# One core: experts' weights split in an order of their own, differential attention's step b moved, modulation moved behind the merge

## The chip, the cores and the metric

The kernel runs on one core of a Trainium2 chip. The metric is the device time of one execution in microseconds (us); lower is better. The engines have these names in the profile: PE is TensorE (matmuls), PEld its weight loads, DVE is VectorE, ACT is ScalarE, POOL is GpSimd, SP is SyncE, which here only starts transfers. Each engine has its own queue of instructions and works through it in order; semaphores make one wait for another.

## What is computed

A transformer in two parts, all in float32. The first part (`first_block`) has two layers over 1024 tokens and, in the first layer, 256 tokens of context, with a model width of 1024. Reduced to what matters here:

```python
for l in range(2):
    mod = s_c @ ada_w[l] + ada_b[l]                 # six vectors of 1024 for the tokens
    mod_c = s_cc @ ada_w[l] + ada_b[l]              # and six for the context
    hx = rms_norm(x, norm1_g[l]) * (1.0 + sc1) + sh1
    hc = rms_norm(xc, norm1_g[l]) * (1.0 + csc1) + csh1
    y_lat, y_ctx = token_mixers(hx, hc, w_in[l], w_out[l], ...)
    x = x + g1 * y_lat
    x = x + g2 * expert_choice_ffn(rms_norm(x, norm2_g[l]) * (1.0 + sc2) + sh2, ...)
    # layer 0 does the same to the context, with cg1 and cg2

def diff_attn_core(q, k, v, lam):                   # one of the token mixers
    s = einsum('bqhmd,bkhmd->bhmqk', q, k) * (DIFF_D ** -0.5)
    a = softmax(s)
    w = a[:, :, 0] - lam * a[:, :, 1]
    return einsum('bhqk,bkhd->bqhd', w, v)

def expert_choice_ffn(x, router_w, wg, wu, wd):     # 16 experts
    aff = softmax(einsum('bnd,de->bne', x, router_w))
    gate, idx = top_k(aff.transpose(0, 2, 1), cap)  # each expert takes 128 tokens, 32 of the context
    xg = x[bidx, idx]
    hid = silu(einsum('becd,edf->becf', xg, wg)) * einsum('becd,edf->becf', xg, wu)
    o = einsum('becf,efd->becd', hid, wd) * gate[..., None]
    return zeros_like(x).at[bidx, idx].add(o)
```

The second part (a gated delta layer and an attention layer with shared latent keys) is not touched.

## The kernel before, in words

The parts of a layer follow one another: norm_in (modulation, norm and the input products), the mixers (diff attention among them), merge (output products, residual, second norm, router), the ranking of the tokens, and the experts. Inside a part the program is written as small steps, and steps of different work are interleaved by hand: a function is cut into a list of steps or into a generator, and the loop that drives the products pops a step between two groups of matmuls. Each engine runs its instructions in the order in which they were written, apart from what a scheduler with priorities moves; a tile's pool has a number of buffers, and a new tile waits until the oldest buffer is free.

**Modulation.** `ada` makes a stretch of `mod` in blocks of 512 columns. A block has three steps: two `part`s with 16 rows of matmul records between them on TensorE (L166) against a 2 MB piece of `ada_w`, and a `total`, in which ScalarE has copied the four partial sums to `adat` (L169), TensorE adds them up with the matrix `sel4` (L177), VectorE adds the bias tile `adab` (L179), and GpSimd starts the transfer to `modd` in memory (L180). GpSimd also starts the load of the bias (L162). Layer 0's first part is made before and inside norm_in, with one step popped per group of products (columns 2048 to 6144). Layer 1's 12 blocks, 36 steps, are made in layer 0's merge: from tile 3 on a step is popped at four places of each tile, and what remains is popped two at a time between the rounds of the ranking.

**Merge.** A tile is 128 tokens; there are ten in layer 0 (eight and two of context) and eight in layer 1. A tile's products are two times 24 matmuls (L917), and its norm writes h (L938 to L940, the half of it on GpSimd) to memory. The ranking (`best`, `choose`) finds each expert's tokens by rounds on VectorE, and `choose` makes the lists of indices by which GpSimd gathers.

**Diff attention.** A unit is 128 queries of one head; it has two score maps. Step a(m) makes the scores of one map on TensorE (S), their extreme on VectorE (L592, a reduce of 128x1280) and the exponential on ScalarE, which also sums up. Step b makes the factor of the second map on VectorE (L598, L599, both tiny), scales the second map by it (L600), and GpSimd adds the first map to it (L601). Steps c and d transpose and multiply by V. `units` runs them as a pipeline: in each turn a(0) of one unit, b of the unit before, a(1), then c and d of older ones.

**Experts.** For each of 16 experts there are three products (gate, up, down) of 1024x1024 weights. float32 is worked in three passes with a high and a low part: ScalarE copies a weight to `wh` (L1165), and `wl` is the difference (L1166), of which VectorE makes three quarters and GpSimd one, by 128x1024 pieces. `weight` loads half a weight (2 MB, SyncE) and splits it, just ahead of the product that uses it; wh and wl have two buffers of half a weight. `product` runs 48 matmuls of 512 columns (L1187), and in layer 0 also the context's matmuls (L1181, in float32, 32 columns of the array), 16 per half. `fetch` gathers the tokens of the expert after next with GpSimd (L1143), and `scatter` adds the result to memory.

## Time and profile before

| | before |
|---|---|
| median of 3 runs | 4869.98 us (4869.22 to 4873.66) |
| the profiled execution: its own time | 4872.44 us |
| its span, first to last instruction | 4870.5 us |
| mean granted TensorE clock | 0.952 |
| norm_in, layer 0 | 0 to 392 us |
| diff attention, layer 0 | 393 to 604 us |
| merge, layer 0: first to last product | 716 to 902 us |
| ranking and rest of the modulation, layer 0 | 902 to 956 us |
| experts, layer 0 | 956 to 1731 us |
| diff attention, layer 1 | 2049 to 2228 us |
| merge, layer 1: products | 2329 to 2453 us |
| experts, layer 1 | 2513 to 3192 us |

The times of the stages are read from the trace of the profiled execution, in microseconds from the start of its span, and so all of them belong to 4872.44 us and not to the median. Busy time of an engine is the time in which one of its instructions ran; a busy share says nothing by itself, since an engine that is not the last to be waited for may stand idle at no cost. The granted clock is a share of TensorE's full clock of 2.4 GHz.

### The profile page before, as it was taken

Reading aid. Unit: us, or ns where it says so; the run is one execution under the profiler, and the core shown is the slowest. Engines: PE = TensorE matmul, PEld = TensorE weight load, DVE = VectorE, ACT = ScalarE, POOL = GpSimd, SP = SyncE. Lnnn points to the kernel's source line nnn. Section 1 sums busy time; section 2 is a strip of 40 time slices with the busy share of each in tenths; the row PEclk is TensorE's granted clock in tenths of the full one; section 3 lists DMA queues with packets and bytes.
Section 4 is the critical chain, followed back from the end, with each engine's and each line's share of the span. In section 5 each row is a group of like instructions: output and inputs, shape, how many; then the busy total and the mean of one; then the engine's idle time right before and its main releaser. Section 6 shows DMA issues by size and latency. Waiting matters only on the chain.

```text
span 4870.5 us, 77258 instructions
## 1 busy us (share of the span) xinstructions
PE 4427.4 (91%) x30151; PEld 3480.5 (71%) x30151; DVE 3183.5 (65%) x6512; ACT 2225.7 (46%) x4037; POOL 1358.2 (28%) x1033
## 2 busy tenths in 40 slices
PE   8998889799999979989959888879999998898899
PEld 4686676476777757867747666658888876787787
DVE  6536877755555566397778998856666663676551
ACT  3326653255555543376336656643333331454330
POOL 2214502244454422162124444412111100022111
PEclk9999899899999989999979999989999999999999
DMA  6422246687878722313548988821111123146757
GB/s 209 159 89 63 60 140 252 217 295 285 291 285 293 279 87 84 103 48 92 202 160 327 329 320 316 309 95 45 36 36 45 41 61 119 56 169 224 191 151 150
DMA packets 333997, 817.14 MB, mean 168 GB/s; under 512 B 32524, under 2 KB 125380, under 8 KB 333632
## 3 DMA queue, kind: packets, MB, share of 16 engines
q1 hardware_dynamic: 228368, 602.22, 34.2%
q0 software_dynamic: 51520, 125.07, 10.9%
q10 hardware_dynamic: 53744, 84.92, 5.0%
q8 instruction: 237, 3.88, 0.3%
q14 instruction: 128, 1.05, 0.1%
HBM read 690.47 MB, written 121.66 MB: 167 GB/s over the span
## 4 chain that ended last, share of the span: by engine, by line
PE 30%; DVE 8%; issue 5%; ACT 4%; DMA 3%; POOL 1%; SPq 0%; ACTq 0%; POOLq 0%; DVEq 0%
PE ps_z L1358 8%; PE ps_m L1187 5%; DVE wl L1166 4%; ACT wh L1165 2%; PE ps_mm L2211 2%; PE ps_S L2119 2%; PE ps_t L2147 1%; PE ps_m L917 1%; PE ps_i L1680 1%; PE ps_i L1694 1%; PE ps_m L1854 1%; PE ps_i L1687 1%; POOL wl L1166 1%; PE ps_t L1482 1%; PE ps_o L1599 1%
## 5 line engine op out<-in xcount | busy, mean ns | idle before, releaser
L1166 DVE TENSOR_TENSOR wl<-w,wh 128x1024 fp32r<-128x1024 f32 x576 | 843.5, 1508 | 179.7 <-ACT wh L1165 179.7
L1165 ACT ACTIVATE wh<-w 128x1024 fp32r<-128x1024 f32 x768 | 754.6, 1050 | 264.0 <-PE ps_m L1187 151.5
L1166 POOL TENSOR_TENSOR wl<-w,wh 128x1024 fp32r<-128x1024 f32 x192 | 535.7, 2825 | 634.9 <-ACT wh L1165 571.1
L1187 PE MATMUL ps_m<-wl,xTh 128*128 128x512 f32 x1024 | 344.6, 411 | 49.0 <-DVE wl L1166 33.6
L1187 PE MATMUL ps_m<-wh,xTh 128*128 128x512 f32 x1024 | 336.2, 410 | 1.4 <-ACT xTh L1133 1.4
L376 PE MATMUL ps_mm<-wh,hh 128*128 128x256 f32 (+1 forms) x928 | 322.5, 350 | 9.3 <-ACT wh L313 6.1
L1187 PE MATMUL ps_m<-wh,xTl 128*128 128x512 f32 x1024 | 325.1, 399 | 0.0
L376 PE MATMUL ps_mm<-wl,hh 128*128 128x256 f32 (+1 forms) x928 | 317.9, 344 | 2.7 <-DVE wl L314 2.6
L376 PE MATMUL ps_mm<-wh,hl 128*128 128x256 f32 (+1 forms) x928 | 316.1, 342 | 0.0
L1358 PE MATMUL ps_z<-hh,wh 128*128 128x350 f32 (+2 forms) x792 | 277.5, 351 | 2.0 <-ACT hh L1291 1.2
L1187 PEld LDWEIGHTS ps_m<-wl,xTh 128*128 128x128 f32 x1024 | 190.0, 192 | 114.4 <-DVE wl L1166 51.9
L1358 PE MATMUL ps_z<-hl,wh 128*128 128x350 f32 (+3 forms) x792 | 268.1, 339 | 0.0
L1358 PE MATMUL ps_z<-hh,wl 128*128 128x350 f32 (+2 forms) x792 | 264.5, 334 | 0.0
L601 POOL TENSOR_TENSOR e<-e,e 128x1280 f32<-128x1280 f32 (+1 forms) x72 | 191.6, 2661 | 188.2 <-DVE e L600 154.8
L1187 PEld LDWEIGHTS ps_m<-wh,xTh 128*128 128x128 f32 x1024 | 188.0, 192 | 64.2 <-issue 14.4
L1187 PEld LDWEIGHTS ps_m<-wh,xTl 128*128 128x128 f32 x1024 | 195.1, 192 | 41.3
L592 DVE TENSOR_REDUCE mx<-ps_S 128x1 f32<-128x1280 f32 (+1 forms) x144 | 196.1, 1366 | 37.0 <-PE ps_S L591 36.3
L376 PEld LDWEIGHTS ps_mm<-wh,hh 128*128 128x128 f32 x928 | 177.3, 192 | 48.0 <-issue 11.0
L376 PEld LDWEIGHTS ps_mm<-wl,hh 128*128 128x128 f32 x928 | 178.5, 192 | 22.4 <-DVE wl L314 4.4
L594 ACT ACTIVATE e<-ps_S,mx 128x1280 f32<-128x1280 f32 (+1 forms) x144 | 177.4, 1233 | 33.2 <-DVE mx L592 22.0
L376 PEld LDWEIGHTS ps_mm<-wh,hl 128*128 128x128 f32 x928 | 177.5, 192 | 18.8 <-issue 0.8
L1187 PE MATMUL ps_m<-wl,hTh 128*128 128x512 f32 x512 | 165.0, 403 | 20.5 <-DVE wl L1166 12.7
(661 smaller groups left out, 10754.0 us busy)
## 6 DMA issues: line engine op xcount, KB each, us to landing
w<-in_exp_w_gate SPq DMA_DIRECT2D x64, 2048.0 KB
w<-in_exp_w_up SPq DMA_DIRECT2D x64, 2048.0 KB
w<-in_exp_w_down SPq DMA_DIRECT2D x64, 2048.0 KB
w<-in_ada_w SPq DMA_DIRECT2D x12, 2048.0 KB
z<-zd POOLq DMA_DIRECT2D x76, 320.0 KB, 4.6
wraw<-in_ada_w SPq DMA_DIRECT2D x38, 512.0 KB
zd<-hi ACTq DMA_DIRECT2D x76, 256.0 KB
zw<-in_t_win SPq DMA_DIRECT2D x64, 256.0 KB
```

What stands on the lines that cost most here:

```text
L376: nc.tensor.matmul(pm[:, o:], hs[i][x][:, k, a * 128:(a + 1) * 128], w[:, k % 2, o:], start=q == 0, stop=q == 23)
L592: nc.vector.tensor_reduce(U["mx"][:, m:m + 1], S[:, :nk], AX.X, OP.min)
L594: nc.scalar.activation(e[:, :nk], S[:, :nk], AF.Exp, scale=-1.0, bias=U["mx"][:, m:m + 1], accum_out=U["sm"][:, m:m + 1])
L601: nc.gpsimd.tensor_add(w[:, :nk], w[:, :nk], U[0][:, :nk])
L917: nc.tensor.matmul(pm, a[:, k], b[:, k], start=k + x == 0, stop=k == 7 and x == 2)
L1165: nc.scalar.activation(wh[:, k], w[:, k], AF.Copy)
L1166: (nc.gpsimd if k == 3 else nc.vector).tensor_sub(wl[:, k], w[:, k], wh[:, k].bitcast(F32))
L1187: nc.tensor.matmul(pm[:, c], X[i][:, half * 4 + k], W[j][:, k, c * 512:(c + 1) * 512], start=half + k + q == 0, stop=half == 1 and k == 3 ...
L1358: nc.tensor.matmul(q[:M, :n], a[:, k % 4], b[:, k, z0:z0 + n], start=k == 0 and x == 0, stop=k == 7 and x == 2)
L1482: nc.tensor.transpose(pt[:r, i * 128:(i + 1) * 128], src[:, tok(t0 + i)[1]], self.ident)
L2119: nc.tensor.matmul(S[:, ks], q[:, i * 128:(i + 1) * 128], k[:, ks], start=x == 0, stop=x == 4)
L2211: nc.tensor.matmul(pm[:, c], a[:, k], b[:, k, c * 512:(c + 1) * 512], start=k + z == 0, stop=k == 7 and z == 2)
```

## The change

There are three edits, in three parts of the first block.

**Modulation.** The block of columns 5120 to 6144 of layer 0 (two blocks of 512) leaves norm_in and is made in the merge, ahead of layer 1's twelve; so 14 blocks, 42 steps, are there instead of 36. Steps are popped between products only from tile 8 on, eight of them; 34 run in the loop behind the last tile. With `late`, the bias is added by a second small matmul with the identity (L180 after), ScalarE copies the sum out (L181), the first `part` of a block is put ahead of the `total` of the block before, the partial sums alternate between the PSUM banks "a" and "m", and the bias tile has two buffers.

**Diff attention.** a(1) moves ahead of b in a turn, and in b the scalar_tensor_tensor and the scaling are issued behind the reduce of a(1) of the next unit (`issue_after`).

**Experts.** A queue `todo` of weight pieces in the order of the products takes the place of `weight`. `split` loads and splits one piece: in layer 0 half a weight, one piece ahead, with two buffers; in layer 1 a quarter (256 rows), three pieces ahead, with five buffers. wl is made on VectorE alone, in 128x2048 pieces, and ScalarE's copy has that shape too. In layer 0 the context's matmuls of both halves run together when a product begins. In layer 1 the bank of the context's sums goes to the transposes, which then have two.

Lines of the kernel after are 4 to 10 larger up to the merge and the gather, and some 25 to 31 larger in the experts: L592 becomes L598, L599 L607, L600 L608, L629 L637, L632 L640, L180 (the store) L184, L940 L948, L1134 L1144, L1143 L1153, L1166 L1191, L1181 L1212, L1197 L1228, L1204 L1235, L1219 L1250.

```diff
-    def ada(self, l, c0, c1, W, load, p, ps, tag, cols=None):
+    def ada(self, l, c0, c1, W, load, p, ps, tag, cols=None, late=False):
...
-                cur["pa"] = ps(tag)
+                cur["pa"] = ps((tag, "m")[late and j // W % 2])
                 if cols is None:
-                    b = cur["b"] = p.tile([2, W], F32, name="adab", bufs=2 if l else 1)
+                    b = cur["b"] = p.tile([2, W], F32, name="adab", bufs=2 if l or late else 1)
...
-            nc.tensor.matmul(pb[:2, :n], self.sel4, cur["t"][:, :n], start=True, stop=True)
+            pb = ps("m" if late else tag)
             b = cur["b"]
-            nc.vector.tensor_add(b[:, :n], pb[:2, :n], b[:, :n])
+            nc.tensor.matmul(pb[:2, :n], self.sel4, cur["t"][:, :n], start=True, stop=not late)
+            if late:
+                nc.tensor.matmul(pb[:2, :n], self.ident[:2, :2], b[:, :n], start=False, stop=True)
+                nc.scalar.activation(b[:, :n], pb[:2, :n], AF.Copy)
+            else:
+                nc.vector.tensor_add(b[:, :n], pb[:2, :n], b[:, :n])
             nc.gpsimd.dma_start(self.modd[l][:, j:j + n], b[:, :n])
...
+            at = len(steps) - 1 if late and steps else len(steps)
+            steps[at:at] = g[:1]
+            steps += g[1:]
...
-        steps = self.ada(0, 2048, 6144, CW, ada_load, p, ps, "mm") if l == 0 else []
+        steps = self.ada(0, 2048, 5120, CW, ada_load, p, ps, "mm") if l == 0 else []
...
                 old[0]["a"](0)
+                old[0]["a"](1)
             if old[1]:
-                old[1]["b"]()
-            if old[0]:
-                old[0]["a"](1)
+                old[1]["b"](old[0] and old[0].get("max"))
...
-            nc.vector.scalar_tensor_tensor(sm[:, 3:4], sm[:, 3:4], self.nlam, sm[:, 0:1], op0=OP.mult, op1=OP.mult)
-            nc.vector.tensor_scalar(w[:, :nk], w[:, :nk], sm[:, 3:4], None, op0=OP.mult)
+            with self.tc.issue_after(behind) if behind else nullcontext():
+                nc.vector.scalar_tensor_tensor(sm[:, 3:4], sm[:, 3:4], self.nlam, sm[:, 0:1], op0=OP.mult, op1=OP.mult)
+                nc.vector.tensor_scalar(w[:, :nk], w[:, :nk], sm[:, 3:4], None, op0=OP.mult)
...
-                ada = self.ada(1, 0, 6144, 512, ada_load, p, ps, "a")
+                for x, c0 in ((0, 5120), (1, 0)):
+                    ada += self.ada(x, c0, 6144, 512, lambda j, n, i, x=x: ada_load(j, n, i, x), p, ps, "a", late=True)
...
-                            if ada and t >= 3 and n in (0, 3, 4, 7):
+                            if ada and t >= 8 and n in (0, 3, 4, 7):
...
-        with self.pool("ex") as p, self.banks("exps", m=3, c=1, t=1) as ps:
+        with self.pool("ex") as p, self.banks("exps", m=3, **(dict(c=1, t=1) if ctx else dict(t=2))) as ps:
...
-                wh, wl = [p.tile([128, 4, 1024], F32R, name=f"w{b}", bufs=2) for b in "hl"]
-                for k in range(4):
-                    nc.scalar.activation(wh[:, k], w[:, k], AF.Copy)
-                    (nc.gpsimd if k == 3 else nc.vector).tensor_sub(wl[:, k], w[:, k], wh[:, k].bitcast(F32))
...
+            G, ahead = (4, 1) if ctx else (2, 3)
...
+            todo = [(name, e, k) for name, e in order for k in range(0, 8, G)]
+            ready = []
+            def split():
...
+                name, e, k = todo.pop(0)
+                if k % 4 == 0:
+                    self.wraw = self.wr.tile([128, 4, 1024], F32, name="w", tag="w")
+                    nc.sync.dma_start(self.wraw, A[name][l, e, k * 128:(k + 4) * 128].rearrange("(k p) f -> p k f", p=128))
+                w = self.wraw[:, k % 4:k % 4 + G]
+                wh, wl = [p.tile([128, G, 1024], F32R, name=f"w{b}", bufs=ahead + (1 if ctx else 2)) for b in "hl"]
+                for i in range(0, G, 2):
+                    nc.scalar.activation(wh[:, i:i + 2], w[:, i:i + 2], AF.Copy)
+                    nc.vector.tensor_sub(wl[:, i:i + 2], w[:, i:i + 2], wh[:, i:i + 2].bitcast(F32))
+                ready.append((w, wh, wl))
...
+                for s in range(0, 8, G):
+                    w, *W = weight()
+                    if ctx and s == 0:
                         pc = U[key + "c"] = ps("c")
-                    for k in range(4 if ctx else 0):
-                        b = half * 4 + k
-                        for g in range(4):
...
+                        for b in range(8):
+                            v = (w, ready[0][0])[b // 4]
+                            for g in range(4):
...
```

**VectorE in layer 1's diff attention.** The rows are in VectorE's order; mx and sm hold a unit's extremes and sums, e a score map. Before, at a place in the middle:

```order
L600 TENSOR_SCALAR e_18593<-e_18593,sm 128x1280
L592 TENSOR_REDUCE mx<-ps_S 128x1
L598 RECIPROCAL sm<-sm 128x2
L599 SCALAR_TENSOR_TENSOR sm<-sm,nlam 128x1
L592 TENSOR_REDUCE mx<-ps_S 128x1
L600 TENSOR_SCALAR e_18645<-e_18645,sm 128x1280
L629 COPY oT<-ps_t 128x128
L592 TENSOR_REDUCE mx<-ps_S 128x1
L632 TENSOR_SCALAR Y<-ps_t,sm 128x64 x2
L598 RECIPROCAL sm<-sm 128x2
L592 TENSOR_REDUCE mx<-ps_S 128x1
```

After, at the same place:

```order
L608 TENSOR_SCALAR e_18207<-e_18207,sm 128x1280
L598 TENSOR_REDUCE mx<-ps_S 128x1
L604 RECIPROCAL sm<-sm 128x2
L598 TENSOR_REDUCE mx<-ps_S 128x1
L607 SCALAR_TENSOR_TENSOR sm<-sm,nlam 128x1
L637 COPY oT<-ps_t 128x128
L608 TENSOR_SCALAR e_18259<-e_18259,sm 128x1280
L640 TENSOR_SCALAR Y<-ps_t,sm 128x64 x2
L598 TENSOR_REDUCE mx<-ps_S 128x1 x2
L604 RECIPROCAL sm<-sm 128x2
L607 SCALAR_TENSOR_TENSOR sm<-sm,nlam 128x1
```

Before, one reduce stands between a scaling and the next scalar_tensor_tensor in one turn and two in the next; after, two stand there in every turn.

**VectorE in layer 1's experts.** rd is an expert's result on its way to memory, ag the hidden values, xTl and hTl low parts of the transposed tokens and hidden values. From one result before:

```order
L1219 SCALAR_TENSOR_TENSOR rd<-ps_m,gate_22018,g_22030 128x1024
L1166 TENSOR_TENSOR wl<-w,wh 128x1024 x2
L1134 TENSOR_TENSOR xTl<-ps_t,xTh 128x512
L1166 TENSOR_TENSOR wl<-w,wh 128x1024 x6
L1204 TENSOR_TENSOR ag<-ag,ps_m 128x512 x2
L1134 TENSOR_TENSOR hTl<-ps_t,hTh 128x512
L1166 TENSOR_TENSOR wl<-w,wh 128x1024 x3
L1134 TENSOR_TENSOR hTl<-ps_t,hTh 128x512
L1166 TENSOR_TENSOR wl<-w,wh 128x1024 x2
L1197 SCALAR_TENSOR_TENSOR ag<-ag,ps_m 128x1024
L1166 TENSOR_TENSOR wl<-w,wh 128x1024
```

And after:

```order
L1250 SCALAR_TENSOR_TENSOR rd<-ps_m,gate_21636,g_21648 128x1024
L1191 TENSOR_TENSOR wl<-w,wh 128x2048 x4
L1235 TENSOR_TENSOR ag<-ag,ps_m 128x512 x2
L1191 TENSOR_TENSOR wl<-w,wh 128x2048 x2
L1144 TENSOR_TENSOR hTl<-ps_t,hTh 128x512 x2
L1191 TENSOR_TENSOR wl<-w,wh 128x2048 x2
L1228 SCALAR_TENSOR_TENSOR ag<-ag,ps_m 128x1024
L1144 TENSOR_TENSOR xTl<-ps_t,xTh 128x512 x2
L1191 TENSOR_TENSOR wl<-w,wh 128x2048 x4
```

An expert has 18 subtracts of 128x1024 on VectorE before (and six on GpSimd, not shown), and 12 of 128x2048 after.

**GpSimd between layer 0's merge and the first gather.** modd is the modulation in memory, adab the bias tile, h and x belong to the merge's tiles. Before, from the last tiles on:

```order
L925 TENSOR_TENSOR x<-x,o 128x512
L180 DMA modd_78<-adab 2x512
L162 DMA adab<-in_ada_b 2x512
L180 DMA modd_78<-adab 2x512
L162 DMA adab<-in_ada_b 2x512
L180 DMA modd_78<-adab 2x512
L940 TENSOR_TENSOR h<-h,B_8227 128x512
L180 DMA modd_78<-adab 2x512
L1143 DMA x<-hd,idx_8681 128x1024
```

After, the rows ahead of the gather; seven more such pairs of store and load stand above them, and the last h above those:

```order
L184 DMA modd_78<-adab 2x512
L162 DMA adab<-in_ada_b 2x512
L184 DMA modd_78<-adab 2x512 x2
L1153 DMA x<-hd,idx_8683 128x1024
L1153 DMA xc<-hc,idx_8687 128x256
```

Before, one store stands between the last h and the gather; after, ten stores and eight loads of bias stand there.

## Rows read from the trace of the kernel before

**Rows 1.** The page's first part: busy time, share of the span, instructions.

```profile
PE 4427.4 (91%) x30151; PEld 3480.5 (71%) x30151; DVE 3183.5 (65%) x6512; ACT 2225.7 (46%) x4037; POOL 1358.2 (28%) x1033
```

**Rows 2.** Busy times by stage: window, length, engines, clock, DMA share, GB/s.

```profile
716.00:902.00 186.00, 179.72 (x928) 123.79 (x927) 129.61 (x353) 56.02 (x115) 38.60 (x39) 0.98 0.72 262
902.00:956.00 54.00, 22.23 (x110) 8.71 (x109) 42.55 (x128) 7.75 (x16) 8.41 (x10) 0.61 0.57 199
956.00:1731.00 775.00, 772.60 (x5694) 543.19 (x5694) 448.59 (x461) 438.11 (x510) 373.77 (x155) 1.00 0.78 278
2513.00:3192.00 679.00, 600.46 (x2557) 458.54 (x2557) 593.37 (x413) 414.63 (x462) 289.46 (x124) 0.97 0.85 311
```

**Rows 3.** Waits, 2520 to 3185: waiter, releaser, us, times, longest.

```profile
PE ps_m L1187 <- DVE wl L1166: 46.3, 41, 4.2
...
PE ps_m L1187 <- POOL wl L1166: 23.2, 39, 2.0
```

**Rows 4.** Groups by line and form, same stretch: busy us, mean ns.

```profile
L1166 DVE TENSOR_TENSOR wl<-w,wh 128x1024 fp32r<-128x1024 f32 x281 | 493.5, 1806 | 19.5 <-ACT wh L1165 19.5
```

**Rows 5.** One line's instructions, same stretch: ns minimum, median, maximum.

```profile
L1166 DVE TENSOR_TENSOR wl<-w,wh x281: 1207/1218/6758, 2522.8 to 3184.5; 128x1024 fp32r<-128x1024 f32 x141
```

**Rows 6.** Timeline, GpSimd and VectorE, 2732 to 2752: start, length in us, instruction.

```profile
2734.96 5.29 POOL L1166 TENSOR_TENSOR wl<-w,wh 128x1024 fp32r<-128x1024 f32 x2
2743.27 2.57 POOL L1166 TENSOR_TENSOR wl<-w,wh 128x1024 fp32r<-128x1024 f32 x1 [3.02 <-ACT wh L1165]
...
2735.68 13.52 DVE L1166 TENSOR_TENSOR wl<-w,wh 128x1024 fp32r<-128x1024 f32 x6
```

**Rows 7.** Timeline of TensorE in layer 0's experts, behind a context batch.

```profile
1201.83 0.73 PE L1187 MATMUL ps_m<-wh,hTh 128*128 128x512 f32 x2
1202.40 0.62 PE L1187 MATMUL ps_m<-wl,hTh 128*128 128x512 f32 x2
```

**Rows 8.** Groups by line: diff attention of layer 0, layer 1, and GpSimd's add.

```profile
L599 DVE SCALAR_TENSOR_TENSOR sm<-sm,nlam 128x1 f32<-128x1 f32 x40 | 24.8, 621 | 0.5
...
L599 DVE SCALAR_TENSOR_TENSOR sm<-sm,nlam 128x1 f32<-128x1 f32 x32 | 25.6, 801 | 0.6
...
L601 POOL TENSOR_TENSOR e<-e,e 128x1280 f32<-128x1280 f32 x29 | 84.1, 2902 | 63.9 <-DVE e L600 48.3 <-PE ps_t L625 6.1 <-PE ps_t L615 5.7
```

**Rows 9.** Timelines of VectorE in the diff attention of layer 1 and layer 0.

```profile
2106.93 1.48 DVE L592 TENSOR_REDUCE mx<-ps_S 128x1 f32<-128x1280 f32 x1
...
2108.53 1.60 DVE L599 SCALAR_TENSOR_TENSOR sm<-sm,nlam 128x1 f32<-128x1 f32 x1
...
2116.79 1.48 DVE L592 TENSOR_REDUCE mx<-ps_S 128x1 f32<-128x1280 f32 x1
...
491.40 1.48 DVE L592 TENSOR_REDUCE mx<-ps_S 128x1 f32<-128x1280 f32 x1
...
500.28 1.48 DVE L592 TENSOR_REDUCE mx<-ps_S 128x1 f32<-128x1280 f32 x1
```

**Rows 10.** Windows of the merge's products alone (L917): five tiles, four tiles.

```profile
766.50:866.30 99.80, 66.19 (x241) 42.05 (x241) 1.00 0.62 224
2379.80:2440.40 60.60, 50.24 (x193) 34.30 (x193) 1.00 0.30 105
```

**Rows 11.** Timeline of GpSimd from the merge's end to the first gather.

```profile
898.88 0.53 POOL L180 DMA_DIRECT2D modd<-adab  x1 [1.52 <-DVE adab L179]
903.91 0.53 POOL L162 DMA_DIRECT2D adab<-in_ada_b  x1 [4.50 <-DMA modd<-adab]
...
920.23 1.66 POOL L940 TENSOR_TENSOR h<-h,B 128x512 f32<-128x512 f32 x1 [1.44 <-issue]
...
949.37 1.04 POOL L1143 DMA_INDIRECT x<-hd,idx  x1 [23.54 <-DVE gate L1106]
```

**Rows 12.** Timeline of TensorE behind the merge: one block of modulation.

```profile
910.97 3.64 PE L166 MATMUL ps_a<-w,csT 128*32 128x512 f32 x16 [2.89 <-DVE adab L179]
915.39 1.86 PE L177 MATMUL ps_a<-adat,sel 128*2 128x512 f32 x2 [0.78 <-ACT adat L169]
```

More of the change, by code (lines that the diff above doesn't have):

```diff
@@ L1 @@
 import math
-from contextlib import ExitStack, contextmanager
+from contextlib import ExitStack, contextmanager, nullcontext
 from itertools import chain
@@ L169, in part, with total @@
                 nc.scalar.activation(t[:, :n], pa[:, :n], AF.Copy)
-        def total(j, n):
+        def total(cur, j, n):
             if cols is not None:
@@ L183, in ada @@
             n = min(W, c1 - j)
-            steps += [lambda j=j, n=n: part(j, n, 0), lambda j=j, n=n: part(j, n, 1), lambda j=j, n=n: total(j, n)]
+            g = [lambda f=f, cur=cur, j=j, n=n, h=h: f(cur, j, n, *h) for cur in [{}] for f, h in ((part, (0,)), (part, (1,)), (total, ()))]
+            at = len(steps) - 1 if late and steps else len(steps)
+            steps[at:at] = g[:1]
+            steps += g[1:]
         return steps
@@ L673, in a, with b @@
             nc.scalar.activation(e[:, n:n + 256], S[:, 768:], AF.Exp, bias=m, accum_out=sm[:, 2:3])
-        def b():
+        def b(behind):
             sm = U["sm"]
@@ L1169, in product @@
-            def product(U, key, x, name, e):
+            G, ahead = (4, 1) if ctx else (2, 3)
+            order = [("exp_w_gate", 0), ("exp_w_up", 0)]
+            for e in range(NE):
+                order += [("exp_w_gate", e + 1)] * (e + 1 < NE) + [("exp_w_down", e)] + [("exp_w_up", e + 1)] * (e + 1 < NE)
+            todo = [(name, e, k) for name, e in order for k in range(0, 8, G)]
+            ready = []
+            def split():
+                if not todo:
+                    return
+                name, e, k = todo.pop(0)
[8 more added lines that the diff above has]
+                ready.append((w, wh, wl))
@@ L1171, in product, with weight @@
+            def weight():
+                split()
+                return ready.pop(0)
+            for _ in range(ahead):
+                split()
+            def product(U, key, x):
                 pm = U[key] = ps("m", 2)
-                pc = None
                 X = U[x]
-                for half in range(2):
-                    w, *W = weight(name, e, half)
-                    if ctx and half == 0:
+                for s in range(0, 8, G):
+                    w, *W = weight()
+                    if ctx and s == 0:
@@ L1185, in product @@
+                    for k in range(G):
+                        b = s + k
                         for q, (i, j) in enumerate(((0, 0), (0, 1), (1, 0))):
                             for c in range(2):
-                                nc.tensor.matmul(pm[:, c], X[i][:, half * 4 + k], W[j][:, k, c * 512:(c + 1) * 512],
-                                                 start=half + k + q == 0, stop=half == 1 and k == 3 and q == 2)
+                                nc.tensor.matmul(pm[:, c], X[i][:, b], W[j][:, k, c * 512:(c + 1) * 512],
+                                                 start=b + q == 0, stop=b == 7 and q == 2)
@@ L1232, in experts @@
                 f()
-            run(product(E[0], "g", "xT", "exp_w_gate", 0), [], 0)
+            run(product(E[0], "g", "xT"), [], 0)
             silu(E[0])
-            run(product(E[0], "u", "xT", "exp_w_up", 0), fetch(1), 0)
+            run(product(E[0], "u", "xT"), fetch(1), 0)
             for e in range(NE):
@@ L1239, in experts @@
                 if e + 1 < NE:
-                    run(product(E[e + 1], "g", "xT", "exp_w_gate", e + 1), steps, 1)
+                    run(product(E[e + 1], "g", "xT"), steps, 1)
                     silu(E[e + 1])
@@ L1244, in experts @@
                         f()
-                run(product(U, "d", "hT", "exp_w_down", e), [], 0)
+                run(product(U, "d", "hT"), [], 0)
                 scatter(U, e)
                 if e + 1 < NE:
-                    run(product(E[e + 1], "u", "xT", "exp_w_up", e + 1), fetch(e + 2) if e + 2 < NE else [], 0)
+                    run(product(E[e + 1], "u", "xT"), fetch(e + 2) if e + 2 < NE else [], 0)
     def h_src(self, t):
```

26 lines of the change are left out of this document (9 added, 17 removed).

## The prediction, made before the changed kernel ran

> **What bounds the kernel now.** I read the page first, then a table of busy times by stage, then, in each stage that the change touches, the waits and the timeline. TensorE is busy for 91% of the span [rows 1], but that is a mean over stages with different limits, and each has to be looked at by itself [rows 2]. In layer 0's experts (775 us) TensorE works for 772.6 us at full clock, so nothing but less TensorE work can shorten them. In layer 1's experts (679 us) it works for only 600.46 us, while VectorE is busy for 593.37 and DMA has a share of 0.85: three engines are near full, and the waits tell which one ends last. They name the low parts of the weights: TensorE waited 46.3 us for wl from VectorE and 23.2 us for wl from GpSimd [rows 3], together 69.5 of its 78.5 us without work. The merge of layer 0 (186 us) is bound by TensorE too (179.72 busy), and the 54 us behind it, in which the tokens are ranked, are a chain of small steps at a granted clock of 0.61. In the diff attention the limit is a loop between TensorE, VectorE, ScalarE and GpSimd, and I read it from VectorE's rows below.
>
> **Layer 1's experts: -66 us.** Every weight is split into wh and wl. 384 subtracts of 128x1024 make wl; GpSimd has every fourth. VectorE's took 1806 ns in the mean [rows 4], but their minimum is 1207 and their median 1218 [rows 5]. So a minority is very long, and the timeline shows where: beside two subtracts of GpSimd (5.29 us) and a third (2.57) VectorE's run of six took 13.52 us instead of 6 x 1.218 = 7.3, and the excess of 6.2 is most of GpSimd's time in that stretch [rows 6]. The two engines subtract one after the other, and handing a quarter to GpSimd buys little: 281 x (1.806 - 1.218) = 165 us of VectorE's time went into waiting. After the change VectorE does all, in 192 pieces of 128x2048, for which I take twice the median, 2.44 us: 468 us. What else it did here is at most 593.37 - 493.5 = 100 us, so VectorE's floor is 568. TensorE's is its 600.46 us at a clock of 0.97, 582 at full clock. DMA's is 0.85 x 679 = 577. All three now lie below the present 679, and the deeper ring (five pieces of 256 rows instead of two of 512, made three ahead) is what lets them approach it. I give back nearly all of TensorE's wait for wl, 66 of 69.5, which gives 613, 5% above the highest floor. Bounds: half of the wait (-35), if the three hand over badly, and -90, near the floor of 582.
>
> The row says that the queues moved 311 GB/s at a share of 0.85, which is 366 GB/s if they were full. The Trainium skill, page "SBUF — State Buffer", section "🎯 Summary: rules for kernel authors", tells authors to reckon a transfer between HBM and SBUF with about 358 GB/s; by that estimate the stage's bytes need 311 x 679 / 358 = 590 us, and no ring makes it shorter, so it would gain 89 at most. By the rows' own rate it is 577 and TensorE's 582 comes first. My 613 stands above both.
>
> **Layer 0's experts: -10 us.** The context's matmuls (32 columns) now run as one batch per product, 32 matmuls, where there were two of 16: 48 batches instead of 96. A switch costs a little: the two matmuls of 512 columns behind a batch took 0.73 us, the next two 0.62 [rows 7], 0.11 more; with as much taken for the entry, 48 x 0.2 = 10 us, all on TensorE's path. Bounds 0 and -14 (entry twice as dear). A batch now needs both halves of a weight when it begins; DMA's share of 0.78 leaves it room, and a half is loaded ahead. The quarter of subtracts that comes to VectorE, 96 x 1.2 = 115 us, fits into the 775 - 449 us in which it was idle [rows 2]. If that cover were gone, each late half would cost its matmuls' wait, as in layer 1.
>
> **Diff attention, both layers: -26 us.** Step b scales a 128x1280 tile on VectorE, and GpSimd adds to it (2.9 us) [rows 8]. The next b's first scalar_tensor_tensor (L599), which works on 128x1, takes about 0.21 us when free, but in the mean it took 621 ns in layer 0 (40 of them) and 801 ns in layer 1 (32) [rows 8]: 40 x 0.41 + 32 x 0.59 = 35 us over. One that took 1.60 us stands in [rows 9]. It started 1.6 us behind the reduce that follows a scaling (2106.93) and ended 3.2 behind it (2110.13); an add that began with that reduce would have ended 2.9 behind it. Before, one or two reduces of 1.48 us stand between a scaling and the next L599; after, always two (the order rows show it). Two take 2.96 us, as long as the add, so the scalar step meets a free GpSimd. Of what is gained there only a part comes back, since other steps of the loop move up. A pair of units with one long L599 lasted from 2106.93 to 2116.79, 9.86 us; two without lasted from 491.40 to 500.28, 8.88 [rows 9]: 0.98 of 1.39 us, 71%, or 25 us of 35; I take 26. Bounds -36 (all of it) and -12 (a third). The cost of the new order is that VectorE's scaling, and so the add and the transposes behind it, come up to one reduce later; the units have two stages of slack until the transposes.
>
> **norm_in of layer 0: -7 us.** Two blocks of modulation (six steps) leave. A step's price comes from the merge, where the only difference between the layers is this work: five tiles lasted 99.8 us with four steps each in layer 0, four tiles 60.6 us without in layer 1 [rows 10], so (19.96 - 15.15) / 4 = 1.2 us. Bounds -3 (ScalarE's and DMA's waits hide some) and -9.
>
> **Merge and ranking of layer 0: +7 us.** Tiles 3 to 7 lose 20 steps, 20 x 1.2 = -24; in tiles 8 and 9 the bias matmuls and a shared PSUM bank add 3 by estimate. The last product then ends at 881 instead of 902. But 14 blocks now run almost wholly behind it, ten of their stores later than the last tile's h. On GpSimd, store of block j and load of bias j+2 alternate, since the bias tile has two buffers, and the load waits for the store to land: 898.88 to 903.91, 5.03 us, and its own 0.53 [rows 11]. So a block takes 5.6 us on that queue. The h of the last tile stands ahead of the first of ten stores; it started 18 us behind the last product (920.23 against 902) and took 1.66. Hence ten stores, nine of them one behind the other at 5.6, the last two adjacent: 20 + 8 x 5.6 + 5 = 70 us behind the last product. Only then comes the gather of expert 0, which now stands at 949.37 [rows 11], and from it 6.6 us to the first product at 956 [rows 2]. TensorE at the low clock needs 3.64 + 1.86 and another 1.86 for the bias, 7.4 us a block [rows 12], more than 5.6; over eight blocks that is up to 14, I take 6. Sum: 881 + 70 + 6.6 + 6 = 963 against 956. Bounds +18 (the low clock all along) and -7 (stores land as fast as in the quickest case and the loads are not waited for). The ranking on VectorE and the 12 additions of bias that leave it lie beside this.
>
> **Sum.** -66 - 10 - 26 - 7 + 7 = -102. The profiled execution lasted 4872.44 us, which gives 4770; the median of the runs is 2.5 lower, and so I predict 4768. Everything from layer 1's end on (3192 us and later) keeps its code.
>
> **Rivals.**
> - R1, slower: VectorE's subtracts are stretched by the traffic of the memory and not by GpSimd. Then all 384 cost 1.806 us, 693 + 100 = 793 for the stage, +114 instead of -66, and the time is about 4948. For it: DMA's share is high. Against it: half the subtracts of the same window are at 1.218 or less [rows 5], at the same traffic. It decides from 3.2 us per 128x2048 piece on, (679 + 36 - 100) / 192, where 36 is what the other terms gain. It is also the case that the change does not do what it says.
> - R2: layer 1's experts are held by hand-overs, since three engines stand at 85 to 90%; a piece that comes late is not made up, and only 30 us come back. 4804.
> - R3: the ring lets them reach TensorE's floor of 582, and 2 more: -95. 4739. By the skill's 358 GB/s it would stop at 590, and the time would be 4745.
> - R4: the tail behind the merge is longer by 25 us, because the low clock and GpSimd's queue add up and do not overlap. 4793.
> - R5: diff attention gives only 5, because TensorE's scores or ScalarE's exponentials end last once the scalar step is short. 4789.
>
> **How the numbers follow.** The forecast has a chance of 0.50 (its own range 4745 to 4795), R1 0.06, R2 0.15, R3 0.11, R4 0.10, R5 0.08. The range of 4714 to 4815 takes in R2 to R5; its low end is the sum of all low bounds (-90 - 14 - 36 - 9 - 7 = -156 from 4870), its high end R2 with the tail at its bound of +18, 11 more than taken. Left out are R1 and the mishaps that add up. A change of 0.2%, about 10 us, is what measuring this kernel can tell from none. Only R1 reaches that far: slower 0.05, same 0.01, faster 0.94.
>
> **What would show it.** The 128x2048 subtract in layer 1 has a mean of 2.4 us or less, and TensorE's wait for wl is below 10 us (right), or a mean above 3 (R1). The stage lasts 600 to 625 us; if it is longer, the wait that is left names the culprit: ScalarE's wh, DMA's w or PSUM. All L599 (L607 after) take 0.21 us; if the diff attention does not shrink by about 13 us in each layer all the same, R5 holds. Merge tiles 3 to 7 of layer 0 last 15.2 us each. GpSimd's rows between the last product and the first gather show ten stores, each waiting about 5 us behind the one before, and the first expert product comes at 963 less what norm_in and diff attention gained by then (7 and 12), at about 944. My prediction is wrong if the long VectorE subtracts stay, or if the modulation held back costs far more than the 28 us it frees.

## The result and the profile after

The changed kernel takes 4740.28 us (median of 4 runs, 4730.14 to 4746.75) against 4870.88 (median of 4) for the kernel before: a ratio of 0.9729, with a 95% interval of 0.9711 to 0.9748. The prediction was 4768 in a range of 4714 to 4815, so the time fell by 131 us where 103 were forecast.

The profiled execution is the fastest of the four (4730.14 us, span 4727.6). The table gives each part's length in it, from the first or last TensorE instruction of one part to that of the next, and the change forecast for it. The parts that the edits don't touch add up to 10 us less than in the profile before. This execution is also 10 us below its median, so I count these 10 us to no edit; how much of that difference lies in the other rows is not known.

| part | before | after | change | forecast |
|---|---|---|---|---|
| up to the first score of layer 0 (norm_in) | 392.5 | 379.1 | -13.4 | -7 |
| diff attention, layer 0 | 211.2 | 198.8 | -12.4 | -12 |
| merge's products, layer 0 | 186.3 | 165.9 | -20.4 | -21 |
| from there to the first expert product | 53.3 | 84.5 | +31.2 | +28 |
| experts, layer 0 | 775.2 | 755.3 | -19.9 | -10 |
| diff attention, layer 1 | 178.0 | 170.9 | -7.1 | -14 |
| experts, layer 1 | 678.2 | 587.7 | -90.5 | -66 |
| all other parts | 2395.8 | 2385.4 | -10.4 | 0 |

The page's first part, and then busy times by stage with the columns of [rows 2] (length, PE, PEld, DVE, ACT, POOL, clock, DMA share, GB/s):

```profile
PE 4363.2 (92%) x30179; PEld 3478.2 (74%) x30179; DVE 3164.8 (67%) x6306; ACT 2197.5 (46%) x3667; POOL 910.5 (19%) x841
```

```profile
689.00:855.00 166.00, 159.67 (x817) 122.30 (x815) 121.38 (x352) 52.65 (x110) 31.94 (x26) 0.98 0.58 213
855.00:939.60 84.60, 61.47 (x286) 13.87 (x284) 38.81 (x117) 21.64 (x37) 19.51 (x27) 0.85 0.92 335
939.60:1695.00 755.40, 751.77 (x5694) 554.70 (x5694) 538.97 (x366) 421.26 (x320) 132.26 (x59) 0.99 0.79 285
2463.60:3051.30 587.70, 566.27 (x2554) 459.04 (x2553) 514.59 (x317) 397.51 (x270) 84.66 (x29) 0.99 0.97 359
```

Layer 1's experts moved from a DMA share of 0.85 to 0.97, and VectorE does more of the subtracts in less busy time (514.59 us against 593.37 [rows 2]). The stretch behind the merge is longer by what the prediction said, and is itself nearly full of transfers (0.92).

Waits of layer 1's experts, 2470 to 3045 (waiter, releaser, us, times, longest), to be read beside [rows 3]:

```profile
ACT wh L1190 <- DMA w<-in_exp_w_gate: 61.4, 24, 4.3
...
ACT wh L1190 <- DMA w<-in_exp_w_up: 51.7, 29, 4.2
...
ACT wh L1190 <- DMA w<-in_exp_w_down: 20.5, 16, 4.6
...
PE ps_m L1218 <- DVE wl L1191: 14.7, 22, 1.4
```

TensorE's wait for wl has gone from 69.5 to 14.7 us, and a new one stands at the head of the line: ScalarE waits 134 us for weights to land. So the transfers seem to end last now; an experiment below asks whether they do. The subtract itself, minimum, median and maximum in ns, in the same stretch, where [rows 5] had 1207/1218/6758 for half the columns:

```profile
L1191 DVE TENSOR_TENSOR wl<-w,wh x188: 2276/2283/2296, 2468.4 to 3035.5; 128x2048 fp32r<-128x2048 f32 x188
```

### The profile page after: what moved, and what is told of

The parts are those of the page before. It is cut to its first block, busy times and chain, and to the rows that moved or that the text cites. A ratio compares the mean times of both kernels' runs of the same rounds, so it can differ in the third digit from the quotient of the medians.

```text
span 4727.6 us, 76129 instructions
## 1 busy us (share of the span) xinstructions
PE 4363.2 (92%) x30179; PEld 3478.2 (74%) x30179; DVE 3164.8 (67%) x6306; ACT 2197.5 (46%) x3667; POOL 910.5 (19%) x841
## 4 chain that ended last, share of the span: by engine, by line
PE 27%; DVE 9%; DMA 7%; issue 6%; ACT 2%; POOL 0%; ACTq 0%; SPq 0%; POOLq 0%; DVEq 0%
PE ps_z L1389 8%; DVE wl L1191 4%; DMA w<-in_exp_w_gate 2%; PE ps_mm L2242 2%; PE ps_S L2150 2%; DMA w<-in_exp_w_down 2%; PE ps_t L2178 1%; PE ps_m L1218 1%; PE ps_m L925 1%; PE ps_m L1885 1%; PE ps_i L1725 1%; PE ps_i L1711 1%; PE ps_i L1718 1%; ACT wh L1190 1%; PE ps_t L1513 1%
## 5 line engine op out<-in xcount | busy, mean ns | idle before, releaser
L1191 DVE TENSOR_TENSOR wl<-w,wh 128x2048 fp32r<-128x2048 f32 x384 | 862.2, 2285 | 241.1 <-ACT wh L1190 240.8
L1190 ACT ACTIVATE wh<-w 128x2048 fp32r<-128x2048 f32 x384 | 717.7, 1910 | 319.2 <-PE ps_m L1218 175.2
L1218 PE MATMUL ps_m<-wl,xTh 128*128 128x512 f32 x1024 | 325.0, 396 | 7.4 <-DVE wl L1191 7.2
L1218 PEld LDWEIGHTS ps_m<-wl,xTh 128*128 128x128 f32 x1024 | 190.9, 189 | 52.5 <-DVE wl L1191 13.4
L598 DVE TENSOR_REDUCE mx<-ps_S 128x1 f32<-128x1280 f32 (+1 forms) x144 | 195.8, 1368 | 42.6 <-PE ps_S L597 42.1
L1251 POOL DMA_INDIRECT xd<-rd,idx x32 | 112.7, 3522 | 419.8 <-DVE rd L1250 376.6
L600 ACT ACTIVATE e<-ps_S,mx 128x1280 f32<-128x1280 f32 (+1 forms) x144 | 177.6, 1235 | 26.6 <-DVE mx L598 19.3
```

The source lines that it names most:

```text
L598: U["max"] = nc.vector.tensor_reduce(U["mx"][:, m:m + 1], S[:, :nk], AX.X, OP.min).ins
L600: nc.scalar.activation(e[:, :nk], S[:, :nk], AF.Exp, scale=-1.0, bias=U["mx"][:, m:m + 1], accum_out=U["sm"][:, m:m + 1])
L1190: nc.scalar.activation(wh[:, i:i + 2], w[:, i:i + 2], AF.Copy)
L1191: nc.vector.tensor_sub(wl[:, i:i + 2], w[:, i:i + 2], wh[:, i:i + 2].bitcast(F32))
L1218: nc.tensor.matmul(pm[:, c], X[i][:, b], W[j][:, k, c * 512:(c + 1) * 512], start=b + q == 0, stop=b == 7 and q == 2)
L1251: nc.gpsimd.indirect_dma_start(out=dst, out_offset=bass.IndirectOffsetOnAxis(ap=idx[:, e:e + 1], axis=0), in_=r, in_offset=None, compute_o ...
```

## The experiments

For the stages the profile of each run is used, since one stage differs little between executions where nothing disturbs it: layer 1's experts lie between 583.4 and 589.8 us in nine profiles with their code as changed.

**What made layer 1's experts faster: GpSimd's quarter, the ring, or the longer pieces.** The theory is the prediction's, that VectorE and GpSimd subtract one after the other; the rival, that the deeper ring brings the time. The kernel before with one edit (128x1024 pieces and the old ring stay; layer 0 has it too):

```diff
-                    (nc.gpsimd if k == 3 else nc.vector).tensor_sub(wl[:, k], w[:, k], wh[:, k].bitcast(F32))
+                    nc.vector.tensor_sub(wl[:, k], w[:, k], wh[:, k].bitcast(F32))
```

> The kernel before, with GpSimd's quarter of the weight subtracts given to VectorE in both layers' experts; pieces of 128x1024 and the ring of two halves stay. Theory A (the engines subtract one after the other; taking GpSimd out is what gained): layer 1's experts fall from 679 us to 610 to 630, since VectorE needs 384 x 1.22 + 100 = 568 us, and all its subtracts take 1.22 us. Theory B (the deeper ring is what gained): the stage stays at 660 to 680, because a wl is still made too late for its product. Rival R1 (memory traffic stretches the subtracts): mean 1.8 us for all 384, stage about 790.

One run took 4779.52 us, beside one of 4866.92 for the kernel before. Layer 1's experts lasted 588.5 us, layer 0's 774.9. Busy times of the stage in layer 1, and its subtracts:

```profile
2509.50:3098.00 588.50, 569.91 (x2557) 452.61 (x2557) 531.83 (x509) 417.00 (x461) 47.35 (x29) 1.00 0.97 359
```

```profile
L1166 DVE TENSOR_TENSOR wl<-w,wh x368: 1212/1218/1228, 2502.0 to 3067.3; 128x1024 fp32r<-128x1024 f32 x184
```

No subtract is longer than 1.228 us where the longest was 6.758, at a higher rate of transfers than before (359 against 311 GB/s). So R1 falls, and this one edit has all of the stage's gain. The trace of the kernel before shows the same piece by piece: of the 281 subtracts of VectorE in [rows 5], the 132 that no subtract of GpSimd's overlaps take 1.226 us at most, and each of the 75 that take over 1.3 us lies beside subtracts of GpSimd's for at least as long as it is late. Two edits of the kernel after are the counterparts. In one, GpSimd takes a quarter again beside the deep ring:

```diff
-                    nc.vector.tensor_sub(wl[:, i:i + 2], w[:, i:i + 2], wh[:, i:i + 2].bitcast(F32))
+                    if ctx or k % 4 == 0:
+                        nc.vector.tensor_sub(wl[:, i:i + 2], w[:, i:i + 2], wh[:, i:i + 2].bitcast(F32))
+                    else:
+                        for o, eng in ((0, nc.vector), (1, nc.gpsimd)):
+                            eng.tensor_sub(wl[:, i + o], w[:, i + o], wh[:, i + o].bitcast(F32))
```

> The kernel after, but in layer 1's experts GpSimd again makes every fourth 128x1024 of wl; the ring of five quarters stays. Theory A: VectorE's 128x1024 subtracts become long again beside GpSimd's, mean 2 us or more for those, and the stage returns to 640 to 680 us from 588. Theory B: the ring absorbs it, and the stage stays at 588 to 600.

The stage came to 633.7 us, 46 more than after (just below the range that the theory gave). Its busy times, and groups by line and form (busy us, mean ns):

```profile
2485.10:3118.80 633.70, 575.99 (x2554) 456.58 (x2553) 601.26 (x317) 398.02 (x270) 357.02 (x124) 0.99 0.92 333
```

```profile
L1192 DVE TENSOR_TENSOR wl<-w,wh 128x2048 fp32r<-128x2048 f32 x94 | 309.1, 3288 | 17.8 <-ACT wh L1190 17.8
L1195 POOL TENSOR_TENSOR wl<-w,wh 128x1024 fp32r<-128x1024 f32 x95 | 289.6, 3095 | 196.3 <-ACT wh L1190 193.3 <-issue 2.5 <-POOL wl L1195 0.3
L1195 DVE TENSOR_TENSOR wl<-w,wh 128x1024 fp32r<-128x1024 f32 x95 | 208.9, 2199 | 0.7 <-ACT wh L1190 0.7
```

VectorE's pieces are long again, 3288 ns for 2283 and 2199 for 1218. In the other, the ring is short:

```diff
-            G, ahead = (4, 1) if ctx else (2, 3)
+            G, ahead = 4, 1
...
-                wh, wl = [p.tile([128, G, 1024], F32R, name=f"w{b}", bufs=ahead + (1 if ctx else 2)) for b in "hl"]
+                wh, wl = [p.tile([128, G, 1024], F32R, name=f"w{b}", bufs=2) for b in "hl"]
```

> The kernel after, but layer 1's experts split half a weight at a time, one ahead, with two buffers, as layer 0's do. Theory A: the stage is 590 to 615 us, at most 25 over the 588 of the deep ring. Theory B: 640 to 680 us.

The stage took 586.1 us, the same as with the deep ring:

```profile
2476.10:3062.20 586.10, 565.70 (x2554) 458.99 (x2553) 516.53 (x317) 399.86 (x271) 79.71 (x29) 0.99 0.97 360
```

The ring gains nothing once VectorE subtracts alone. Beside GpSimd's quarter something else of the change did help, since 633.7 is 45 below the 678 of before: the ring, the longer pieces, the order of `todo` or the second bank for the transposes; no run tells them apart.

**What ends last there now.** Half of the loads are left out, and each first half of a weight is used twice, so the kernel computes something else with the same work of the engines:

```diff
-                if k % 4 == 0:
+                if k % (4 if ctx else 8) == 0:
                     self.wraw = self.wr.tile([128, 4, 1024], F32, name="w", tag="w")
```

> The kernel after, but in layer 1's experts only the first half of every weight is loaded, and the second half's work is done on it again; so half of the bytes are left out, and all work of the engines stays. Theory C (transfers are what ends last in the stage now: share 0.97 at 359 GB/s, ScalarE waits 134 us for weights): the stage falls from 588 us to TensorE's or VectorE's own time, 565 to 575, and ScalarE's waits for the weights go below 20 us. Theory D (TensorE at its floor, 566 busy of 588, and the hand-overs hold it): it stays at 583 to 590.

The stage fell to 557.0 us, 8 below what theory C gave, and in it TensorE is busy nearly all the time; ScalarE no longer waits for weights:

```profile
2477.70:3034.70 557.00, 554.75 (x2554) 458.62 (x2553) 520.27 (x317) 406.61 (x270) 91.20 (x29) 1.00 0.59 198
```

So transfers hold the stage at 588, and TensorE's floor is 557, 25 below the 582 that the prediction had worked out from busy time and clock.

**The batches of layer 0's experts.** Two batches of 16 matmuls per product again:

```diff
-                    if ctx and s == 0:
-                        pc = U[key + "c"] = ps("c")
-                        for b in range(8):
-                            v = (w, ready[0][0])[b // 4]
+                    if ctx:
+                        if s == 0:
+                            pc = U[key + "c"] = ps("c")
+                        for b in range(s, s + 4):
+                            v = w
```

> The kernel after with the context's matmuls of layer 0's experts in two batches of 16 per product again. Theory K (a batch's entry and exit cost TensorE 0.35 us, 48 times): layer 0's experts rise from 755 to 771 to 775 us. The prediction's 0.2 us a batch would give 765. Theory L (the steps that the ring and VectorE's subtracts moved, transposes of the tokens among them, gained the rest): it rises by 10 at most.

The stage lasted 769.6 us, 14.3 more: 0.30 us for each of 48 batches, between the two figures and between the ranges of the two theories.

```profile
952.50:1722.00 769.50, 766.33 (x5693) 548.75 (x5693) 543.23 (x365) 423.15 (x320) 77.79 (x59) 0.99 0.81 279
```

The 5.6 us that are left to 775.2 are not the subtracts, since VectorE alone left the stage at 774.9 in the first run. Before, transposes of the tokens and of the hidden values (15 of each) stood inside batches and cut 30 of them; after, and in this run, none does. That is read from the order of TensorE's instructions. It is a likely cause of the 5.6 us, but no run has it alone.

**The diff attention.** The old order in the kernel after:

```diff
                 old[0]["a"](0)
-                old[0]["a"](1)
             if old[1]:
-                old[1]["b"](old[0] and old[0].get("max"))
+                old[1]["b"](None)
+            if old[0]:
+                old[0]["a"](1)
```

> The kernel after with the diff attention's order of before (a of map 0, b of the unit before, a of map 1). By the prediction's term the two layers together are 26 us longer again; by the stages of the profiles so far it is 7 us in layer 1 (171 against 178) and 5 to 7 in layer 0, 12 to 14 together, and the long scalar_tensor_tensor come back (20 us or more in layer 1).

4753.34 us (ratio to before 0.9754, 0.9738 to 0.9771), 13 us over the kernel after by the medians; the two intervals overlap, so the size of this difference is uncertain. Layer 1 took 176.3 us against 170.9. The tiny steps of layer 1 (lines L607 after, L608 here; busy us, mean ns), in the kernel after and in this run:

```profile
L607 DVE SCALAR_TENSOR_TENSOR sm<-sm,nlam 128x1 f32<-128x1 f32 x32 | 8.5, 267 | 0.3
```

```profile
L608 DVE SCALAR_TENSOR_TENSOR sm<-sm,nlam 128x1 f32<-128x1 f32 x32 | 26.0, 812 | 0.6
```

So the order takes 17.5 us of waiting out of layer 1's VectorE, and 5 to 7 of them come back. Where the others went is asked by leaving out GpSimd's add in both orders; the result is then another one, and everything else is still done:

```diff
-            nc.gpsimd.tensor_add(w[:, :nk], w[:, :nk], U[0][:, :nk])
```

> The kernel after without GpSimd's add of the two score maps in the diff attention, so that the weights are those of the second map alone. No scalar_tensor_tensor can then wait for GpSimd. Theory G (what is left is the loop of scores, extreme and exponential over two PSUM buffers, and GpSimd is no longer on the path): layer 1's diff attention stays at 168 to 171 us. Theory H (GpSimd's add, 2.9 us a unit, still ends last at the transposes or the tiny steps): it falls to 160 or less.

> The old order of the diff attention, also without GpSimd's add. Theory G: layer 1's diff attention is again 165 to 171 us, as with the new order, so 7 to 10 us are all that the long scalar_tensor_tensor ever cost on the path, though they sum to 18. Theory H, and the prediction's 71%: 160 to 165, 13 us or more below the 178 of the old order with the add.

Layer 1's diff attention took 167.8 us with the new order and 166.6 with the old one. With no add to wait for, the order makes no difference, and all that the add ever cost there is 178.0 - 166.6 = 11 us; the new order leaves 3 of them. That is theory G. In layer 0 the add still costs: 186.3 and 191.4 us without it, at granted clocks of 0.98 and 0.93, against 198.8 to 209.1 with it and the new order, at 0.95 to 0.84. The two with the nearest clocks (191.4 and 198.8) differ by 7 us. The tiny steps still sum to 22.5 us there, 24.8 before [rows 8]:

```profile
L607 DVE SCALAR_TENSOR_TENSOR sm<-sm,nlam 128x1 f32<-128x1 f32 x40 | 22.5, 561 | 0.3
```

The long ones (eight, 1.2 to 2.7 us) all stand beside the units with 256 keys, whose reduces are short (about 0.4 us) and leave the add uncovered. One ends with GpSimd's add; both rows are of the kernel after, by start and length:

```profile
468.88 2.90 POOL L609 TENSOR_TENSOR e<-e,e 128x1280 f32<-128x1280 f32 x1 [1.32 <-DVE sm L604]
469.13 2.66 DVE L607 SCALAR_TENSOR_TENSOR sm<-sm,nlam 128x1 f32<-128x1 f32 x1
```

**The stretch behind the merge.** Theory E: GpSimd's queue sets it; F: the transfers of the modulation's weights. The bias rows of all blocks are loaded once, so that no load stands between two stores:

```diff
...
-                nc.tensor.matmul(pb[:2, :n], self.ident[:2, :2], b[:, :n], start=False, stop=True)
+                i = cur["i"]
+                nc.tensor.matmul(pb[:2, :n], self.ident[:28, i:28:14], late[0][:28], start=False, stop=True)
...
+                late = [p.tile([128, 512], F32, name="ada" + i) for i in "io"]
+                for x, r, c0 in ((1, 0, 0), (1, 14, 0), (0, 12, 5120), (0, 26, 5120)):
+                    n = (6144 - c0) // 512
+                    nc.gpsimd.dma_start(late[0][r:r + n], A["ada_b"][x, c0:6144].rearrange("(b f) -> b f", f=512))
```

> The kernel after, but the bias rows of all 14 late blocks are loaded once ahead of the merge into one tile of 28 rows, a block's two rows are picked by columns of the identity, and the sums go to a tile of their own; so GpSimd issues stores alone, and none waits behind a load. Theory E (the queue of GpSimd, in which each load waits for a store to land, sets the 84.5 us between the last product of the merge and the first expert product): the stretch falls by 8 to 25 us, to 60 to 76. Theory F (the transfers of the 2 MB pieces of the modulation's weights set it: DMA share 0.92 in the stretch): it stays at 79 to 86.

The stretch took 77.5 us. In the eight profiles with the change's own modulation it lies between 84.5 and 93.9, 89.3 in the mean; so 7 to 16 come out, 12 against the mean. 77.5 lies between the ranges of the two theories: GpSimd's queue sets a part of the stretch. What is left points to F, since the share of DMA is 0.95 now (863 to 942 of this run), but no run takes these transfers out.

```profile
863.00:942.00 79.00, 57.88 (x295) 14.77 (x293) 40.60 (x121) 21.62 (x37) 11.44 (x17) 0.90 0.95 350
```

The kernel's time, 4737.51 us (ratio 0.9732, 0.9716 to 0.9748), can't be told from that of the change. Steps from tile 6 on, alone and with the bias loaded once:

```diff
-                            if ada and t >= 8 and n in (0, 3, 4, 7):
+                            if ada and t >= 6 and n in (0, 3, 4, 7):
```

> The kernel after, but steps of the modulation are popped between products from tile 6 on, not from tile 8 on: eight more steps beside products, eight fewer behind them. Theory E: the merge's products last 8 x 1.2 = 10 us longer, and the stretch behind shrinks by 8/3 blocks of 5.3 us = 14; together -4. Theory F gives about the same, since the weights are then also loaded earlier: 2.7 x 2.1 MB at 335 GB/s is 17 us less behind, together -7.

> Both edits of the two runs before. Theory E: -15 to -25 us against the kernel after in the merge and the stretch behind it together; Theory F: like the pop from tile 6 alone, -4 to -7.

Products and stretch together are 253.5 us with the first (179.2 + 74.3) and 246.6 with both (179.2 + 67.4). The profile after has 250.4 (165.9 + 84.5), but it has the shortest stretch of the eight, whose sums go from 250.4 to 260.2, 256.2 in the mean. Against that mean the first gains 3 us and both 10, between E and F again, and against the lowest of the eight hardly anything; one profile of each can't settle it. Eight steps cost the products 13.3 us, 1.7 each. The times are 4742.70 (ratio 0.9744, 0.9728 to 0.9760) and 4734.70 us (0.9728, 0.9712 to 0.9744). The second has the lowest median of all kernels here, but its interval is nearly that of the change, so it is not shown to be faster.

**The modulation's edits as a whole.** Undone in the kernel after:

```diff
-        steps = self.ada(0, 2048, 5120, CW, ada_load, p, ps, "mm") if l == 0 else []
+        steps = self.ada(0, 2048, 6144, CW, ada_load, p, ps, "mm") if l == 0 else []
...
-                for x, c0 in ((0, 5120), (1, 0)):
-                    ada += self.ada(x, c0, 6144, 512, lambda j, n, i, x=x: ada_load(j, n, i, x), p, ps, "a", late=True)
+                for x, c0 in ((1, 0),):
+                    ada += self.ada(x, c0, 6144, 512, lambda j, n, i, x=x: ada_load(j, n, i, x), p, ps, "a")
...
-                            if ada and t >= 8 and n in (0, 3, 4, 7):
+                            if ada and t >= 3 and n in (0, 3, 4, 7):
```

> The kernel after without the edits on the modulation: all blocks of layer 0 in norm_in, steps popped from tile 3 on, bias added on VectorE. By the profiles, norm_in lasts 13.5 us longer again, the merge with the stretch behind it 11 us shorter; so the kernel is 0 to 6 us slower than with them. By the prediction's own terms (7 and 7) it would be the same. If it is faster by more than 5, the edit is a loss.

4742.29 us (0.9734, 0.9711 to 0.9757), the same as with them. norm_in, the products and the stretch are 391.2 + 186.9 + 53.3 = 631.4 us without the edits; with them 629.5 in the first profile, and about 635 with the mean stretch.

## Why the prediction was right, and where it missed

**Layer 1's experts: mechanism right, size short (-66 forecast, -90.5 measured).** That the two engines subtract one after the other, and that handing all subtracts to VectorE removes the wait, is shown from both sides, by 588.5 us with that edit alone and 633.7 with GpSimd back. Of the signs named, the subtract came as told (2.283 us), but TensorE's wait for wl is 14.7 us and not below 10, and 587.7 lies below the 600 to 625. The gain just passes the term's bound of 90. Two parts of the term were wrong. I left 5% above the highest floor for hand-overs, and there is less than that: the stage came to within 2% of the 577 worked out for DMA. And I took TensorE's 582 for the highest floor, but 600.46 x 0.97 was not work alone: with the loads halved the same matmuls are 554.75 us of busy time at full clock. That the deeper ring "is what lets them approach it" is false, as the short ring shows. R3 has the right size (-95, and 4739 for the kernel), but not the cause: the ring did nothing, and transfers were the bound, not TensorE's 582. That the kernel's 4740.28 falls beside R3's 4739 is luck, since the other terms are off as well. The Trainium skill's rule for transfers (page "SBUF — State Buffer", section "🎯 Summary: rules for kernel authors", 358 GB/s) gave an estimate of 590, and the stage's 587.7 us at 359 GB/s is close to it; the last section says why that is partly chance.

**Layer 0's experts: mechanism right, size doubled (-10, -19.9).** It is TensorE's path, as its busy time shows (772.6 to 751.8 us). The price of a batch is 0.30 us and not the 0.2 that I took by doubling the exit; 48 times 0.30 already reach the term's bound of 14. 5.6 us come on top, which the prediction didn't look for; the transposes that cut the batches before are their likely cause, not shown alone. That VectorE would have room for GpSimd's quarter holds (538.97 of 755 us busy).

**Diff attention: right in kind, half in size (-26, about -13 by medians whose intervals overlap).** The step that failed is that 71% of the waiting comes back. The pair of units without a long step was taken in layer 0, from 491.40 to 500.28 [rows 9], and in it one of the two scalings is that of a unit with 256 keys. These rows of the kernel before lie within it, the short scaling and a full one:

```profile
495.30 0.35 DVE L600 TENSOR_SCALAR e<-e,sm 128x256 f32<-128x256 f32 x1
...
499.28 0.88 DVE L600 TENSOR_SCALAR e<-e,sm 128x1280 f32<-128x1280 f32 x1
```

So 0.53 of the 0.98 us between the two pairs was that unit's lesser work; 0.45 of 1.39 is left, 32%, which would have given 11 of 35 us. The rest of the time became another wait, as R5 has it: in layer 1 VectorE waits 20.4 us for scores after, 11.5 before, and the runs without the add show that the loop of scores, extreme and exponential takes 167 us in either order. The claim that two reduces cover the add everywhere is wrong beside the 256-key units; in layer 0 the tiny steps give 2.3 us and the scalings 2.4 (33.5 to 31.1), where the term had 16 of waiting. The stage of layer 0 also depends on the granted clock, 0.84 to 0.95 in the profiles with the same code (209.1 and 198.8 us at the two ends), so its -12.4 in the first profile is no measure of the order, and that the forecast had -12 is luck. Three profiles with the old order lasted 208.9 to 211.2 us at 0.86 to 0.88; between 209.1 at 0.84 and 204.3 at 0.90 the new one would lie near 207 there. By that estimate 2 to 5 us are the order's.

**Modulation: right in kind (+28 forecast for the stretch, +31.2 in the first profile, +36 in the mean of eight), norm_in too small (-7, -13.4).** GpSimd's rows from the merge's end to the gather:

```profile
868.91 0.52 POOL L184 DMA_DIRECT2D modd<-adab  x1
873.93 0.52 POOL L162 DMA_DIRECT2D adab<-in_ada_b  x1 [4.50 <-DMA modd<-adab]
874.46 1.28 POOL L948 TENSOR_TENSOR h<-h,B 128x512 f32<-128x512 f32 x1
875.68 0.54 POOL L184 DMA_DIRECT2D modd<-adab  x1
881.27 0.52 POOL L162 DMA_DIRECT2D adab<-in_ada_b  x1 [5.05 <-DMA modd<-adab]
...
929.03 0.52 POOL L184 DMA_DIRECT2D modd<-adab  x1 [3.58 <-ACT adab L181]
929.94 1.04 POOL L1153 DMA_INDIRECT x<-hd,idx  x1 [0.39 <-issue]
```

From 855 to 940 the loads of bias waited 46.0 us for stores in all (us, times, longest):

```profile
POOL adab L162 <- DMA modd<-adab: 46.0, 10, 7.4
```

Each load of a bias waits for a store to land, and the gather starts behind the tenth store, 74.9 us behind the last product, where 70 was worked out, or 76 with the 6 taken for the low clock. The first of the ten left 20.6 us behind the last product, for which the prediction had 20. What I didn't see is how full of transfers the stretch would be (share 0.92); mending the queue returned only part of it. For norm_in, the price of a step was taken from the merge (1.2 us); two blocks cost 12 to 13 us there, 2 and more a step. Why a step is dearer in norm_in was not tried.

## What to carry to other kernels

Before dividing an elementwise step between VectorE and GpSimd, compare the minimum and the mean of its duration in the trace: if the longest ones lie beside the other engine's, the division may be a loss, and handing all of it to VectorE may be most of the gain (87 of 131 us here, from one line, by one run of each kernel). Take the two stretches that a rate is read from with the same shapes in them; one short unit in the reference pair doubled my estimate. And busy time times clock is not a floor while the engine still waits often: only a run that eases the suspected bound showed TensorE's.

## What the runs showed of the hardware

- VectorE's subtract and GpSimd's exclude each other here: 1.218 us becomes 2.199 in the mean with GpSimd's beside it, and GpSimd's takes 3.1. The Trainium skill, page "SBUF — State Buffer", section "Who interferes with whom", says that the two share a pair of ports under an exclusive lock, and that a VectorE instruction with two inputs in SBUF contends with a GpSimd instruction that reads SBUF; the traces agree. What I had not expected is that a scalar_tensor_tensor on 128x1 pays as much as a large one (up to 2.7 us beside an add of 2.9, for 0.21 alone).
- One 128x2048 subtract takes 2.283 us, two of 128x1024 take 2.436: joining saves 0.15 us a pair.
- Layer 1's experts run at 359 GB/s in the mean, but faster in their middle. The page's slices of 118 us:

```profile
GB/s 216 128 92 65 63 155 167 312 296 299 301 299 301 286 101 87 102 52 97 213 118 365 374 382 374 275 47 37 37 46 42 42 61 123 63 176 232 179 161 148
```

  Four slices in a row show 365 to 382 GB/s. So the 358 of the Trainium skill's rule is no ceiling for this core working alone. The stage's mean is lower because its loads end before its last products do: from 3024 us to the stage's end at 3051 the rate is 116 GB/s or less.
